# Both FFN output products as seven products of blocks, with the later modulation in the token mixers

## The chip, the cores and the metric

The kernel runs on one core of a Trainium2 chip. A core has TensorE (PE, matmuls; PEld is its weight load), VectorE (DVE), ScalarE (ACT), GpSimd (POOL) and SyncE (SP). Each takes its own list of instructions in order. Here SP issues all the loads and stores. On-chip memory (SBUF) has 128 partitions; matmuls write to PSUM, which has eight banks of 512 float32 numbers a partition. The metric is the device time of one execution in microseconds (us).

## The reference

One layer works on 1024 latent tokens with 1024 features and on 256 context tokens. It has two half-step SwiGLU FFNs with 2816 hidden features, and token mixers between them.

```
x  = x  + 0.5 * ml[2] * swiglu(modulate(rms_norm(x,  norm1_g), ml[0], ml[1]), ffn1_w_in, ffn1_w_out)
cx = cx + 0.5 * mc[2] * swiglu(modulate(rms_norm(cx, norm1_g), mc[0], mc[1]), ffn1_w_in, ffn1_w_out)
hx = modulate(rms_norm(x, norm2_g), ml[3], ml[4])
...            # short gated convolution and attention on hx @ w_in, merged by gates, one output product
x  = x + ml[5] * merge_branches(...)
x  = x + 0.5 * ml[8] * swiglu(modulate(rms_norm(x, norm3_g), ml[6], ml[7]), ffn2_w_in, ffn2_w_out)
return rms_norm(x, final_g)

def swiglu(h, w_in, w_out):
    a, b = jnp.split(h @ w_in, 2, axis=-1)
    return (jax.nn.silu(a) * b) @ w_out
```

The modulation vectors `ml` and `mc` are nine pieces of 1024 numbers, made from `silu(c) @ w_mod + b_mod`. The output products are the ones with `w_out`: 2816 hidden features to 1024 features, for 1024 tokens.

## The kernel before

Features lie in partitions, as 8 tiles of 128 features (22 hidden tiles in the FFNs); tokens lie along the free dimension, in two chunks of 512, C0 and C1. Every float32 operand is split into two float32r parts, hi and lo: ScalarE copies hi, then VectorE subtracts to get lo. A product of tiles takes three matmuls (hi hi, hi lo, lo hi), accumulated in a PSUM bank.

The kernel is traced by Python code, and a scheduler orders each engine's list by its own estimate of times; a few instructions are pinned to the order of the code. Buffers are rings: 38 tiles of 4 KiB a partition in `apool` (`atile`), 11 small tiles in `tpool` (`ttile`), and in `wpool` three buffers for raw weights ("raw") and four each for two parts ("wh", "wl"). PSUM has five banks for products (`ps_s`), two for transposes (`ps_t`) and one more (`ps_o`).

**Input products.** The class `Winograd` already makes the products with `w_in` of both FFNs and most of the mixers' input products by seven products of 2 x 2 blocks where eight would be usual: two tiles of output columns by two halves of input features, and two halves of features by two halves of tokens. One such pair gives a hidden tile for all 1024 tokens. `lefts` makes the left operands (their sums on GpSimd); `norm0` and `norm1` make the right operands of the two token halves; `first`, `second` and `third` make the seven products and add them up on VectorE.

**First FFN.** The loop over the 22 hidden tiles makes the input products. `spill` applies silu and writes the hidden values to DRAM (`hd`). From tile 8 on, the context's products use the same weights. Between the tiles, `run(steps, ...)` issues steps of `all_later_mods`: each loads a row tile of `w_mod` (`rawm`), multiplies and adds it on VectorE (`macc`); after eight such a half of a modulation vector is summed by two small matmuls and comes back as columns through four tiny transfers (`mcol`).

Then come the output products (lines 1029 to 1066). For each chunk the 22 hidden tiles are loaded and split, and so are the residual rows `x`. Feature tiles are taken in groups of 3, 3 and 2; for each, blocks of 8, 8 and 6 row tiles of `ffn1_w_out` are loaded with `load_w`, for both chunks anew. Four steps of the later modulation follow each block in C0; the rest of them follow the first block of C1. The second norm of C0 (`norms2`) is made in four steps while the products of C1 run. Every finished tile is added to `x` under its gate on VectorE, stored to `xd`, and squared for the second norm (`mix.square`, in order of tiles).

**Mixers.** `mix.start(norm1)` begins five pairs while the norm of C1 is made. A loop over 8 feature tiles makes the convolution's inputs and the gates. Values, keys, queries, attention, and the merge follow, unchanged by what is below.

**Second FFN.** `Winograd.ffn` (lines 742 to 786) takes two hidden tiles at a time: their input products, silu, split, and at once their share of the output products for both chunks (8 feature tiles, 2 hidden tiles, 3 parts), added to `x` under the gate. The hidden values never leave the chip. In the last pair C1 is taken in two halves of 256 tokens, and `after2` lets the final norm of what is finished run between them. `final` squares and sums the features of a chunk, makes the scale, transposes back to tokens and stores.

## Time and profile before

| | before |
|---|---|
| median of 3 runs | 2814.75 us (2810.68 to 2815.31) |
| the profiled execution's own time (its span) | 2813.7 us |
| mean granted TensorE clock in it | 0.984 |
| busy: PE, PEld, DVE, ACT, POOL | 2725.5, 2286.0, 1957.2, 1096.5, 542.3 us |
| instructions on PE | 13741 |
| moved by DMA | 298.77 MB, 106 GB/s on average |

The page gives one profiled execution. Busy times count overlapping pieces once, so a busy TensorE need not run at its peak. "Idle before" in a group of instructions is the time its engine stood still just before them, with the instruction that ended the wait. The chain of waits is followed back from the last instruction, so that its shares add up to the span. All helper calls are recorded at line 88, so that rows are told apart by tile names: `ps<-hid,wh` is an output product of the first FFN, `ps<-hid,wo` and `ps<-gh,wo` one of the second, `raw` are raw weights, `macc` is the later modulation.

### The profile page before, as it was taken

How to read it: one execution, taken by the hardware profiler on the slowest of the kernel's cores; microseconds unless marked ns; L12 is line 12 of the kernel's file. 1: busy time of each engine (PE TensorE's matmuls, PEld its weight loads, DVE VectorE, ACT ScalarE, POOL GpSimd, SP SyncE). 2: the span in 40 equal slices, each digit the busy share in tenths (PEclk: the TensorE clock that was granted, in tenths of full speed). 3: DMA queues.
4: the chain of work that ended last, by engine and by line, in shares of the span. 5: the costliest groups of instructions: out<-in, count | busy, mean ns of one | idle time of the engine just before them, and what ended most of it. 6: DMA issues, size and time to landing. Idle time of an engine off the chain costs nothing.

```text
span 2813.7 us, 37012 instructions
## 1 busy us (share of the span) xinstructions
PE 2725.5 (97%) x13741; PEld 2286.0 (81%) x13741; DVE 1957.2 (70%) x3218; ACT 1096.5 (39%) x2176; POOL 542.3 (19%) x433
## 2 busy tenths in 40 slices
PE   7898999999999989999999999999998999999998
PEld 4687988888888868888999888887886788888887
DVE  5886688877864387676568377776458766666667
ACT  3524333333433243333345167764245222232225
POOL 2541122121001054323123000000014221212111
PEclk8899999999999989999999999999999999999999
DMA  8264433445974333323313300002532311221111
GB/s 303 97 199 151 145 111 126 130 142 158 309 236 130 104 119 106 105 69 97 105 46 122 111 23 5 12 1 90 170 93 90 111 41 51 60 60 53 46 53 68
DMA packets 346910, 298.77 MB, mean 106 GB/s; under 512 B 25430, under 2 KB 276456, under 8 KB 346728
## 3 DMA queue, kind: packets, MB, share of 16 engines
q1 hardware_dynamic: 346728, 296.40, 32.9%
q8 instruction: 108, 1.77, 0.3%
q14 instruction: 74, 0.61, 0.1%
HBM read 247.54 MB, written 48.76 MB: 105 GB/s over the span
## 4 chain that ended last, share of the span: by engine, by line
PE 83%; DVE 9%; DMA 3%; issue 2%; ACT 2%; SPq 0%; POOL 0%; ACTq 0%; DVEq 0%; POOLq 0%
PE ps L88 73%; PE po L88 6%; PE pt L88 4%; DVE wl L88 2%; DVE r L88 1%; DVE nt L88 1%; DVE macc L88 1%; DMA raw<-in_ffn_w_out_dram 1%; DMA rawm<-in_w_mod_dram 1%; DVE wo L88 1%; DMA hid<-hd 1%; DVE h L88 1%; DVE uc L88 0%; SPq L88 0%; DMA mcol<-mrow 0%
## 5 line engine op out<-in xcount | busy, mean ns | idle before, releaser
L88 PE MATMUL ps<-r,wl 128*128 128x512 f32 x5280 | 1242.0, 394 | 36.9 <-ACT wl L88 12.8
L88 PEld LDWEIGHTS ps<-r,wl 128*128 128x128 f32 x5280 | 995.5, 190 | 256.1 <-ACT wl L88 16.4
L88 ACT CAST wl<-s 128x512 fp32r<-128x512 f32 x256 | 158.6, 620 | 330.3 <-PE ps L88 274.5
L88 ACT CAST wl<-raw 128x512 fp32r<-128x512 f32 x230 | 142.3, 620 | 245.7 <-PE ps L88 165.8
L88 DVE TENSOR_TENSOR wl<-raw,wl 128x512 fp32r<-128x512 f32 x228 | 167.1, 733 | 99.9 <-ACT wl L88 98.8
L88 DVE TENSOR_TENSOR wl<-s,wl 128x512 fp32r<-128x512 f32 x256 | 217.4, 850 | 11.6 <-ACT wl L88 9.8
L88 POOL TENSOR_TENSOR s<-raw,s 128x512 f32<-128x512 f32 x64 | 99.1, 1549 | 624.2 <-DVE wl L88 618.9
L88 PE MATMUL ps<-hid,wh 128*128 128x512 f32 x704 | 217.2, 390 | 1.4 <-ACT wh L88 1.4
L88 ACT CAST wh<-raw 128x1024 fp32r<-128x1024 f32 (+2 forms) x100 | 97.9, 982 | 251.5 <-PE ps L88 208.6
L88 DVE SCALAR_TENSOR_TENSOR x<-ps,gate_l,x 128x512 f32<-128x512 f32 (+1 forms) x200 | 140.7, 726 | 79.1 <-PE ps L88 78.8
L88 POOL TENSOR_TENSOR sq_acc<-sq_acc,sq 128x512 f32<-128x512 f32 (+1 forms) x33 | 41.8, 1268 | 765.4 <-ACT sq L88 764.6
L88 POOL TENSOR_TENSOR s<-raw 128x512 f32<-128x512 f32 x64 | 91.2, 1424 | 399.4 <-DMA raw<-in_ffn_w_in_dram 164.5
L88 DVE TENSOR_TENSOR wl<-raw,wh 128x1024 fp32r<-128x1024 f32 (+1 forms) x92 | 109.6, 1192 | 67.5 <-ACT wh L88 65.8
L88 PEld LDWEIGHTS ps<-hid,wh 128*128 128x128 f32 x704 | 131.7, 188 | 30.2 <-ACT wh L88 2.6
L88 DVE SCALAR_TENSOR_TENSOR macc<-rawm,silu_c,macc 128x512 f32<-128x512 f32 x168 | 141.4, 859 | 12.0 <-DMA rawm<-in_w_mod_dram 11.0
L88 PE MATMUL ps<-hid,wo 128*128 128x512 f32 (+1 forms) x552 | 147.7, 381 | 0.4 <-DVE x L88 0.3
L88 DVE TENSOR_TENSOR u<-u,ps 128x512 f32<-128x512 f32 x168 | 114.3, 680 | 46.6 <-PE ps L88 46.3
L88 PE MATMUL ps<-wh,r 128*128 128x256 f32 x768 | 141.5, 285 | 0.0
L88 PE MATMUL ps<-gh,wo 128*128 128x512 f32 (+1 forms) x368 | 135.5, 380 | 1.5 <-ACT wo L88 1.5
L88 PE MATMUL ps<-hid,wl 128*128 128x512 f32 x352 | 136.5, 389 | 0.0
L88 DVE TENSOR_REDUCE m<-ps 128x1 f32<-128x512 f32 (+1 forms) x192 | 112.7, 595 | 20.9 <-PE ps L88 19.8
L88 DVE TENSOR_TENSOR pts<-pt,pts 128x512 fp32r<-128x512 f32 x160 | 108.7, 683 | 18.8 <-ACT pts L88 18.4
(259 smaller groups left out, 4897.1 us busy)
## 6 DMA issues: line engine op xcount, KB each, us to landing
raw<-in_ffn_w_in_dram SPq DMA_DIRECT2D x114, 512.0 KB, 3.7
raw<-in_ffn_w_out_dram SPq DMA_DIRECT2D x76, 512.0 KB, 4.6
rawm<-in_w_mod_dram SPq DMA_DIRECT2D x128, 256.0 KB, 4.1
raw<-in_w_in_dram SPq DMA_DIRECT2D x57, 512.0 KB, 4.0
hid<-hd SPq DMA_DIRECT2D x44, 256.0 KB, 6.2
rawm<-in_w_mod_dram SPq DMA_DIRECT2D x16, 512.0 KB, 8.1
xd<-x SPq DMA_DIRECT2D x32, 256.0 KB, 8.6
x<-xd SPq DMA_DIRECT2D x32, 256.0 KB, 6.1
```

The costliest lines, as they stand in the source:

```text
L88: inst = getattr(self.engine, name)(*args, **kw)
```

## The change

The output products of both FFNs are made by one new function, `row_products`, by seven products of blocks. The blocks of `w_out` are halves of its rows (11 hidden tiles each) by halves of its columns (4 feature tiles each). The blocks of the hidden values are the same halves of hidden tiles by the two chunks. Each product has 11 hidden tiles x 4 feature tiles x 3 parts of matmuls, into four banks, where eight products of that size were made before (1056 matmuls for an FFN, now 924). It goes through the hidden tiles in pairs: one load, one split and one block sum handle two row tiles, 1024 elements a partition; the eleventh tile stands alone.

With upper and lower rows u and l, left and right columns, and tokens 0 and 1, the seven products in order are:

| product | left operand (w_out) | right operand (hidden) | goes to |
|---|---|---|---|
| 1 | W(u, left) | B(u, 0) | kept in `chain` |
| 2 | W(l, left) | B(l, 0) | 1 + 2: left tiles, C0 |
| 5 | S = W(u, right) + W(l, right) | T = B(u, 1) - B(u, 0) | left and right tiles, C1 |
| 6 | S - W(u, left) | B(l, 1) - T | 1 + 6: left tiles, C1 |
| 7 | W(u, left) - W(u, right) | B(l, 1) - B(u, 1) | 1 + 6 + 7: right tiles, C1 |
| 4 | W(l, right) | B(l, 1) - T - B(l, 0) | 1 + 6 + 7 - 4: right tiles, C0 |
| 3 | W(l, left) - (S - W(u, left)) | B(l, 1) | left tiles, C1 |

The block sums are made on VectorE in place, in the code of the product before the one that needs them (product 7's left operand is the exception). S stays on the chip; the other weight blocks are loaded when needed: one load a pair in products 1 and 5, three in product 2, two in 7 and 4, none in 6 and 3. All hidden values of 1024 tokens are held at once, as raw float32 in 22 tiles (`Rows`), and are split again for each product.

The second FFN now makes all its hidden values first, writes them to `hd` with `spill`, and reads them back, as the first does. `Winograd.ffn` goes. In its last product tokens are taken in halves of 256 (`halves=True`); the operands of both halves are kept, and the final norm runs between.

The later modulation's steps leave the first FFN's output products: nine go to each of the mixers' eight rounds, and the rest behind them. The second norm of C0 runs during product 3. The squares of C1 are taken in the order in which tiles get done (4 to 7, then 0 to 3). `final` takes one step a feature tile, scales on VectorE, and for 256 tokens gives the sum on TensorE six partial tiles where VectorE added all up before.

```diff
     class Winograd:
...
         def square(self, d):
-            if d == 0:
+            if not self.n_squares:
                 self.acc = [ttile("sq_acc")]
-            sq = self.acc[0] if d == 0 else ttile("sq")
+            sq = ttile("sq") if self.n_squares else self.acc[0]
             act.activation(out=sq, in_=self.xs(d, C1), func=AF.Square)
...
-        def ffn(self, w_o, gate, last_chunks, after):
...
+    class Rows:
+        def __init__(self, n, name):
...
+        def fetch(self, src):
+            for lower in range(2):
+                for c in range(2):
+                    for k, m in self.groups:
+                        j = lower * self.n + k
+                        load(self.t[k, lower, c], src[j : j + m, :, c * 512 : (c + 1) * 512].rearrange("a p n -> p a n"))
+
+    def row_products(w, rows, add, after=lambda i, k: None, halves=False):
+        R, groups = P * rows.n, rows.groups
+        sums = {}
+
+        def part_of_w(k, m, lower, left):
+            t = wpool.tile([P, 2, 512], F32, tag="raw", name=uniq("raw"), bufs=3)[:, :m]
+            o, c = k * P + R * lower, 512 * (not left)
+            load(t, w[o : o + m * P, c : c + 512].rearrange("(a p) n -> p a n", p=P))
+            return t
...
+        def operands(i, k, m, tags=("wl", "wh")):
+            b11, b12, b21, b22 = (rows.t[k, v, c] for v in range(2) for c in range(2))
+            if i == 1:
+                left = part_of_w(k, m, 0, True)
+            elif i == 2:
+                left = part_of_w(k, m, 1, True)
+            elif i == 7:
+                left, a21 = part_of_w(k, m, 0, True), part_of_w(k, m, 0, False)
+                dve.tensor_sub(out=left, in0=left, in1=a21)
+            elif i == 4:
+                left = part_of_w(k, m, 1, False)
+            else:
+                left = sums[k]
+            right = {1: b11, 2: b21, 5: b11, 6: b11, 7: b12, 4: b11, 3: b22}[i]
+            l, r = parts(left, m, tags[0]), parts(right, m, tags[1])
+            if i == 1:
+                dve.tensor_sub(out=b11, in0=b12, in1=b11)
+            elif i == 2:
+                sums[k] = atile("ws", (P, 2, 512))[:, :m]
+                a21, a22 = part_of_w(k, m, 0, False), part_of_w(k, m, 1, False)
+                dve.tensor_add(out=sums[k], in0=a21, in1=a22)
+            elif i == 5:
+                a11 = part_of_w(k, m, 0, True)
+                dve.tensor_sub(out=sums[k], in0=sums[k], in1=a11)
+                dve.tensor_sub(out=b11, in0=b22, in1=b11)
+            elif i == 6:
+                dve.tensor_sub(out=b12, in0=b22, in1=b12)
+            elif i == 7:
+                dve.tensor_sub(out=b11, in0=b11, in1=b21)
+            elif i == 4:
+                a12 = part_of_w(k, m, 1, True)
+                dve.tensor_sub(out=sums[k], in0=a12, in1=sums[k])
+            return l, r
...
+        for i in (1, 2, 5, 6, 7, 4, 3):
...
+            ps = [ps_s() for _ in range(4)]
+            for k, m in groups:
+                steps_of(ps, k, m, *operands(i, k, m))
+                after(i, k)
+            for d in range(4):
+                if i == 1:
+                    chain[d] = ttile("u")
+                    act.copy(out=chain[d], in_=ps[d])
+                elif i == 2:
+                    c = ttile("c")
+                    dve.tensor_add(out=c, in0=chain[d], in1=ps[d])
+                    add(d, C0, c)
+                elif i == 5:
+                    add(d, C1, ps[d])
+                    add(d + 4, C1, ps[d])
...
-    for ch in (C0, C1):
...
+    hs = Rows(NH // 2, "hid")
+    hs.fetch(hd)
+    for k in range(KD):
+        for ch in (C0, C1):
+            sp.dma_start(out=xs(k, ch), in_=xd[k, :, ch[1] : ch[1] + 512])
...
+        if i == 3 and k in (0, 2, 4, 6):
+            run(norms2, 1)
+
+    row_products(ffn1_w_out[0], hs, add1, after1)
...
         run(normc2, 2)
+        run(steps, 9)
...
+    run(steps)
     for k in range(4):
         mix.part_second(k)
...
-    fast.ffn(ffn2_w_out[0], gate3["l"], last_chunks, after2)
+    fast.start(fast.norm1())
+    for j in range(NH):
+        u, c = fast.next_first()
+        v, b = fast.second(u)
+        spill(c, b, j, C0)
+        spill(*fast.third(u, v), j, C1)
+    hs = Rows(NH // 2, "hid")
+    hs.fetch(hd)
...
+    row_products(ffn2_w_out[0], hs, add3, after3, halves=True)
     run(finals[1])
     run(finals[2])
```

More of the change, by code (lines that the diff above doesn't have):

```diff
@@ L480, in __init__ @@
             self.n_ahead, self.side, self.started, self.n_left = ahead, None, [], 0
+            self.n_squares = 0
             self.source, self.ready = self.lefts(pairs, side_from), []
@@ L1065, in tile_dit_layer @@
                 if ch == C1:
                     mix.square(d)
+        if (i, k) == (7, 0):
+            gain2.update(norm_gain("gain2", 3, "g2"))
+            mix.gain = gain2["l"]
+        if k == NH // 2:
+            if i == 2:
+                done(range(4), C0)
+            elif i == 7:
+                done(range(4, KD), C1)
+            elif i == 4:
+                done(range(4, KD), C0)
+            elif i == 3:
+                done(range(4), C1)
+        if i == 3 and k in (0, 2, 4, 6):
+            run(norms2, 1)
```

181 lines of the change are left out of this document (91 added, 90 removed).

## The prediction

> **What bounds the kernel now.** I read the page first, then the stages (busy time by stretches), then the chain of waits, and last the groups and queues inside the two stages that the change rewrites.
>
> ```profile
> span 2813.7 us, 37012 instructions
> PE 2725.5 (97%) x13741; PEld 2286.0 (81%) x13741; DVE 1957.2 (70%) x3218; ACT 1096.5 (39%) x2176; POOL 542.3 (19%) x433
> PE 83%; DVE 9%; DMA 3%; issue 2%; ACT 2%; SPq 0%; POOL 0%; ACTq 0%; DVEq 0%; POOLq 0%
> ```
>
> TensorE is the bound: 97% busy, and 83% of the chain that ended last is its own work. Below are the stages around the change: the first FFN's output products, the start of the mixers, their main loop, most of the second FFN, and the tail after its last output matmul. Columns: stretch, length, busy time and instruction count by engine (PE, PEld, DVE, ACT, POOL), granted clock, DMA share, GB/s.
>
> ```profile
> 724.00:969.50 245.50, 244.09 (x1082) 200.46 (x1081) 131.79 (x176) 83.55 (x113) 12.64 (x7) 1.00 0.62 197
> 969.50:1064.00 94.50, 82.22 (x330) 63.68 (x329) 78.79 (x118) 40.16 (x71) 45.96 (x31) 0.89 0.33 109
> 1064.00:1405.00 341.00, 341.00 (x1619) 287.34 (x1618) 225.39 (x337) 107.78 (x182) 98.28 (x69) 1.00 0.31 98
> 2200.00:2792.80 592.80, 592.38 (x2651) 491.27 (x2651) 397.36 (x579) 168.88 (x290) 110.03 (x82) 1.00 0.17 52
> 2799.30:2813.70 14.40, 6.25 (x38) 5.11 (x37) 6.80 (x26) 7.76 (x18) 1.45 (x2) 0.79 0.52 211
> ```
>
> Both FFN stages run on TensorE without a gap, at full clock. So fewer matmuls there shorten the kernel one for one, as long as the operands keep coming. The other engines have room: VectorE is busy 131.79 of 245.50 us.
>
> **The matmuls saved.** The first FFN's output products are two groups in the list of instructions on the hidden tiles, and one piece of the chain gives their pace:
>
> ```profile
> L88 PE MATMUL ps<-hid,wh x704: 387/389/499, 724.3 to 968.8; 128*128 128x512 f32 x176
> L88 PE MATMUL ps<-hid,wl x352: 388/389/398, 725.9 to 969.1; 128*128 128x512 f32 x176
> 882.39 89.79 PE ps L88 x396
> ```
>
> That is 1056 matmuls (22 hidden tiles x 8 feature tiles x 2 token halves x 3 parts), at 89.79 / 396 = 0.2267 us each: 239.4 us. Seven block products of 11 x 4 x 3 = 132 make 924, so 132 go, 29.9 us. The second FFN saves as many, but its last product is cut into halves of 256 tokens. Two 256-wide matmuls of its present end start one after another:
>
> ```profile
> 2785.86 0.28 PE L88 MATMUL ps<-gh,wo 128*128 128x256 f32 x1
> 2785.98 0.28 PE L88 MATMUL ps<-gl,wo 128*128 128x256 f32 x1
> ```
>
> At 0.12 us, 264 of them take 31.7 us where 132 wide ones took 29.9 (+1.8); the 96 narrow ones there today cost 11.5 against 10.9 (0.6, which goes). Net 29.9 - 1.8 + 0.6 = 28.7 us. Both FFNs together: -58.6 us if nothing waits.
>
> **VectorE and ScalarE in the new stage.** These groups of the first FFN's output stage carry the prices (count, busy, mean ns):
>
> ```profile
> L88 DVE TENSOR_TENSOR wl<-raw,wh 128x1024 fp32r<-128x1024 f32 x32 | 40.1, 1256 | 21.1 <-ACT wh L88 20.5 <-PE pt L88 0.3
> L88 DVE SCALAR_TENSOR_TENSOR macc<-rawm,silu_c,macc 128x512 f32<-128x512 f32 x28 | 21.0, 749 | 2.8 <-DMA rawm<-in_w_mod_dram 2.3
> L88 DVE SCALAR_TENSOR_TENSOR x<-ps,gate_l,x 128x512 f32<-128x512 f32 x15 | 11.2, 747 | 13.1 <-PE ps L88 13.1
> L88 DVE TENSOR_TENSOR u<-u,ps 128x512 f32<-128x512 f32 x168 | 114.3, 680 | 46.6 <-PE ps L88 46.3
> L88 ACT CAST wh<-raw 128x1024 fp32r<-128x1024 f32 x30 | 31.5, 1051 | 61.0 <-PE ps L88 46.5 <-DMA raw<-in_ffn_w_out_dram 14.4
> ```
>
> A pass over 11 tiles is 5.5 operations of 1024 elements, 5.5 x 1.256 = 6.9 us. Each product needs two passes for the low parts of its operands, and eight passes of block sums are spread over the seven: 22 x 6.9 = 152 us. Emptying PSUM adds 16 x 0.68 + 28 x 0.747 = 32 us. That is 184 of 209.5 us (924 x 0.2267): 88% where it was 54%. Products 5 and 7 carry two passes of sums: 4 x 6.9 + 5.7 (4 x 0.68 + 4 x 0.747) = 33 us against 29.9. ScalarE needs 14 x 5.5 x 1.051 = 81 us, about its 83.55 of now. In the second FFN the splits of the halved last product are issued inside product 4: 5 passes + 5.7 = 40 us there, though the last product then needs next to none.
>
> So VectorE fits on the whole, but runs at most two pairs ahead: each pair takes two of four buffers a side. In the built order, product 5's first pairs stand among 4 sums and 4 additions of the product before (5.7 us), and product 6's second operand behind four additions: 2 x 0.747 each side of a 1.256 block sum. I put 3 us of TensorE idle at the turns into 5 and into 6 and 1 us into each of 7 and 4: 8 us per FFN. Bounds: nothing, since two pairs last 2 x 24 x 0.2267 = 10.9 us, and the whole 5.7 us at each of 4 turns, 23 us; I take it near the lower end because evictions stand ahead of most splits. Product 4 in the second FFN: 40 - 30 = 10 at most, 0 at least; 7 us of slack in product 7's stretch go towards it, so 3. The second norm over the first tokens now falls into product 3 of the first FFN: 2 us, between nothing and the 6 us of its eight multiplications.
>
> **Loads.** The queue's own rows and two stretches (PE, clock, DMA share, GB/s):
>
> ```profile
> raw<-in_ffn_w_out_dram SPq DMA_DIRECT2D x76, 512.0 KB, 4.6
> hid<-hd SPq DMA_DIRECT2D x44, 256.0 KB, 6.2
> 737.37 1.40 SPq L88 DMA_DIRECT2D hd<-u x1
> 730.00:740.00 10.00, 10.00 (x46) 1.00 1.07 368
> 740.00:750.00 10.00, 10.00 (x46) 1.00 1.05 389
> ```
>
> All loads are issued by one queue in order. In the changed order the fourth and fifth weight blocks of product 1 stand around the last spill of hidden values (issued at 737.37 today). The sixth stands behind that spill, the rest of the hidden tiles, seven modulation rows and all sixteen rows of x: 8.75 MB, 23 us at 380 GB/s. TensorE wants it 5 x 24 x 0.2267 = 27.2 us after product 1 starts, at 751.5. If the spill goes out by 725, because VectorE no longer splits 23 hidden tiles ahead of it, the block comes in time; if at 737 as now, at 760 plus about 2 us to split. Between 0 and 11 us; I take 4, as the work in front of the spill on VectorE is gone.
>
> Product 2 wants three blocks for each pair from three buffers (its left operand and two for the sum): one round is a landing (4.6), the sum (1.26) and the issue, about 6.3 us against 5.4 us of matmuls for a pair. Five rounds lose some 4 us (0 if the first pairs are early; 5 x 3.5 = 17 us if the landing is that of a crowded queue, 8.1, the median of the 512 KB modulation rows below). I take 4 in the first FFN, and 2 in the second, where neither x nor modulation is loaded. Its start costs 1: the hidden values there are written out and read back, but the first two pairs were prepared long before.
>
> ```profile
> rawm<-in_w_mod_dram SPq DMA_DIRECT2D x16, 512.0 KB, 8.1
> ```
>
> The second FFN's added spill (44 writes, 44 tiles read back) and extra weight reads, 26 MB against 11.5, run at 52 GB/s today and are hidden; the spill leaves the queue behind each tile's product, and the next weights are two hidden tiles ahead.
>
> **What moves.** About 63 steps of the later modulation leave the first output stage for the mixers, with some 26 operations of 0.749 us, their row loads and three column transfers. VectorE has 341.00 - 225.39 = 116 us free there; the row loads share the queue with the mixers' weights. I charge 2 us (between 0 and the 20 us if each were waited for; TensorE has no idle in that stretch now). At the start of the mixers the last product ends with four additions and four squares where two of each stood: 2 us more on a chain that already binds (969.50 to 1064.00). In the tail, rows 4 to 7 are done before and the squares feed the sum on TensorE directly: -1.5 us of 14.4 (bounds 0 and -4).
>
> **The sum**, against the profiled 2813.7 us: first FFN -29.9 + 8 + 2 + 4 + 4 = -11.9; second -28.7 + 8 + 3 + 2 + 1 = -14.7; +2 +2 -1.5. Together -24.1: 2789.6. The median of the three runs, 2814.75, is 1.05 above that execution; so 2790.6. The three runs lie within 0.2%, and 0.2% (5.6 us) is about what a measurement can tell from no change.
>
> **A clock row to weigh.** When TensorE idled 2.69 us, its clock fell in the next stretch:
>
> ```profile
> 598.46 5.75 PE L88 MATMUL ps<-r,wl 128*128 128x512 f32 x17 [2.69 <-ACT u L88]
> 590.00:600.00 10.00, 7.31 (x42) 0.96 0.30 94
> 600.00:610.00 10.00, 10.00 (x55) 0.87 0.20 58
> ```
>
> 0.04 and 0.13 of 10 us: 1.7 us lost beside the gap. [...] It speaks against this change, which trades an unbroken stage for one with turns.
>
> **The rivals.**
> - All of it is hidden: the pairs in hand cover each turn, and no load is late. Then -58.6 and the other terms: 2756 to 2765, say 2763. For it: VectorE at 88%. Against: products 5 and 7 exceed their own stretch. Chance 0.17.
> - The turns trip the clock: the stalls are as I sum them, but at eight turns of 2 us or more the clock drops too, 8 x 1.7 = 14 us: 2804. The gap of 2.69 us speaks for it, and my turns of 1 us against. Chance 0.13.
> - The supply becomes the bound, on the slower side: three raw buffers, filled in order by one queue, are freed only when VectorE reaches the split or the sum, and VectorE's fixed order waits for late tiles with splits behind it. Where a round is 4.6 + 1.05 + 1.26 + 1.26 = 8.2 us, products 2, 7 and 4 (three, two, two blocks for three buffers) take 8.2, 5.5 and 5.5 us per pair; with the crowded landing of 8.1, 11.7, 7.8 and 7.8: 5.5 x (6.3 + 2.4 + 2.4) = 61 us lost per FFN against 29. Halfway between 29 and 61, at 45 us, it gives 2814.75 + 2 x 16 = 2846. It decides from a loss of 29 us per FFN, a landing of about 6.2 us, which the hidden tiles have today. For it: that row; against: 2 of the 7 products are without loads, and one block per pair runs unhindered today at the same landing. Chance 0.22.
> - Nothing to measure: gain and stalls cancel, about 2814. Chance 0.08.
>
> The forecast itself has 0.40. Faster: 0.40 + 0.17 + 0.13 less 0.02 for its spread, 0.68; same 0.08 and a little, 0.09; slower 0.23. The range runs from 2762, the hidden case, to 2832, halfway into the slower one; the likeliest case alone holds 2775 to 2805.
>
> **What would show it.** Right: 924 matmuls in each output stage, PE idle of 15 to 20 us in the first, named after VectorE's splits at the turns and once after a weight load in product 1 or 2; VectorE near 85% there; the mixers' main loop without idle. Wrong: idle before every pair of products 2, 7 and 4 behind in_ffn_w_out loads (supply), clock below 0.95 in the output stages, idle in the mixers behind the modulation's row loads, or no idle at all (the hidden case).

## The result, and the profile after

The changed kernel takes 2830.7 us (median of 4 runs, 2824.8 to 2832.0) where the kernel before takes 2814.8: a ratio of 1.0057, with a 95% interval of 1.0044 to 1.0069. It is slower by 16 us; a gain of 24 us was forecast. The profiled execution took 2829.55 us.

The head of the page of the changed kernel: span, busy time by engine, and the chain that ended last by engine.

```profile
span 2827.5 us, 36964 instructions
PE 2699.5 (95%) x13625; PEld 2258.4 (80%) x13625; DVE 2038.5 (72%) x3214; ACT 1124.7 (40%) x2148; POOL 536.5 (19%) x424
PE 76%; DVE 11%; DMA 6%; issue 2%; ACT 2%; POOL 1%; SPq 1%; DVEq 0%; ACTq 0%; POOLq 0%
```

TensorE has 26 us less to do, and yet the span grew: its share of the chain fell from 83% to 76%, and VectorE's and the DMAs' rose by two and three points. The stages of the changed kernel (columns as in the table of stages before): first FFN's output products, start of the mixers, their main loop, second FFN's output products, tail.

```profile
724.00:965.00 241.00, 222.64 (x942) 177.79 (x940) 189.84 (x219) 90.06 (x108) 6.32 (x3) 0.97 0.48 166
965.00:1064.00 99.00, 77.72 (x288) 59.16 (x289) 80.89 (x120) 45.48 (x82) 45.84 (x31) 0.83 0.34 110
1064.00:1391.00 327.00, 323.79 (x1424) 265.72 (x1423) 249.06 (x367) 107.65 (x181) 105.08 (x73) 1.00 0.36 114
2567.70:2810.60 242.90, 232.06 (x1126) 193.84 (x1125) 176.14 (x209) 85.81 (x107) 0.00 (x0) 0.96 0.38 129
2810.60:2827.50 16.90, 8.50 (x78) 8.05 (x76) 11.08 (x42) 5.85 (x11) 0.00 (x0) 0.93 0.54 218
```

By the marks of single matmuls the time splits into three:

| stage | before, us | after, us | difference | forecast |
|---|---|---|---|---|
| first FFN's output products (to the last of their matmuls) | 245.2 | 239.6 | -5.6 | -11.9 |
| from there through the mixers (to the first context product) | 406.8 | 427.8 | +21.0 | +4 |
| second FFN to the end of the span | 701.6 | 700.2 | -1.4 | -16.2 (with the tail) |

The stretch between the mixers and the second FFN is the same in both kernels (736.0 and 735.9 us). So the question has two halves: why the two output stages gained 7 us instead of 28, and why the mixers, which the change hardly touches, lost 21.

**The output stages.** The output products' groups of the changed kernel in these two stages (first the first FFN, then the second; busy time, mean of one, idle before):

```profile
L88 PE MATMUL ps<-wh,wl 128*128 128x512 f32 x924 | 220.8, 399 | 17.9 <-DVE wh L88 5.8 <-ACT wl L88 5.2 <-DVE u L88 3.3
...
L88 PE MATMUL ps<-wh,wl 128*128 128x512 f32 x792 | 192.7, 403 | 10.8 <-DVE c L88 4.0 <-DVE u L88 2.5 <-DVE wh L88 2.4
L88 PE MATMUL ps<-kept,kept 128*128 128x256 f32 x264 | 34.7, 290 | 0.0
```

There are 924 matmuls, as forecast, and the idle time is as forecast too: 17.9 us in the first stage (18 in the sum: 8 + 4 + 4 + 2) and 10.8 in the second (14). What the sum lacks is in the busy time. At 0.2267 us the 924 would take 209.5 us and took 220.8 (+11.3); the 792 would take 179.5 and took 192.7 (+13.2); the 264 narrow ones would take 31.7 and took 34.7 (+3.0). By these groups matmuls became slower by 27.5 us in all. Some of that is counted twice, because groups overlap where one follows another: all groups of the two stages sum to 223.6 and 236.7 us, and TensorE was busy 222.44 and 232.06. So some 22 us are lost in slow matmuls. The products of the first FFN one by one show where (5, 6, 7 and 4; stretch, length, TensorE busy and count, granted clock, DMA share, GB/s):

```profile
793.00:828.00 35.00, 31.89 (x132) 0.95 0.47 158
828.00:864.50 36.50, 33.02 (x134) 0.95 0.06 19
864.50:895.20 30.70, 29.76 (x130) 1.00 0.50 167
895.20:931.50 36.30, 33.17 (x133) 0.91 0.55 174
```

And the turns into 6, 7 and 4, on TensorE (start, length, operation, count, idle time before it and who ended that):

```profile
831.08 0.50 PE L88 MATMUL ps<-wh,wl 128*128 128x512 f32 x1 [2.46 <-DVE x L88]
832.21 32.12 PE L88 MATMUL ps<-wh,wl 128*128 128x512 f32 x132 [0.63 <-DVE wh L88]
864.96 29.76 PE L88 MATMUL ps<-wh,wl 128*128 128x512 f32 x130 [0.63 <-DVE wh L88]
897.99 1.39 PE L88 MATMUL ps<-wh,wl 128*128 128x512 f32 x2 [3.26 <-DVE u L88]
899.72 32.46 PE L88 MATMUL ps<-wh,wl 128*128 128x512 f32 x132 [0.34 <-DVE wh L88]
```

Behind a gap of 0.63 us the product runs at 0.229 us a matmul; behind 2.46 or 3.26 us it runs at 0.243 to 0.246, and the granted clock of the stretch is 0.95 and 0.91. Set against product 7, each long gap costs its own length and about another 2 us (132 x 0.014 to 0.017); a run below shows that not all of it is the clock's. What ends the gaps is VectorE emptying the PSUM banks of the product before (x, u).

One long gap is not needed, and the clock doesn't always fall. At the turn into 6 of the second FFN three short gaps stand close together, and the product behind them is slow (granted clock 0.95):

```profile
2668.14 0.49 PE L88 MATMUL ps<-wh,wl 128*128 128x512 f32 x1 [0.55 <-DVE x L88]
2669.46 0.51 PE L88 MATMUL ps<-wh,wl 128*128 128x512 f32 x1 [0.82 <-DVE x L88]
2670.59 32.33 PE L88 MATMUL ps<-wh,wl 128*128 128x512 f32 x132 [0.63 <-DVE wh L88]
```

The same turn in a later run (fewer ones-matmuls, below) has the same three gaps (0.55, 0.81 and 0.62 us), the clock stays at 1.00, and the 132 matmuls take 31.07 us instead of 32.33:

```profile
2667.94 31.07 PE L88 MATMUL ps<-wh,wl 128*128 128x512 f32 x132 [0.62 <-DVE wh L88]
```

**The start of the mixers.** TensorE, before and after, from the end of the output products to the ones-matmuls of the norm over the second 512 tokens (pt<-ones):

```profile
969.30 2.88 PE L88 MATMUL ps<-r,wl 128*128 128x512 f32 x12
972.02 0.28 PE L88 MATMUL pt<-ones,sq_acc 128*128 128x1 f32 x2
972.16 2.99 PE L88 MATMUL ps<-r,wl 128*128 128x512 f32 x12
974.99 0.28 PE L88 MATMUL pt<-ones,sq 128*128 128x1 f32 x2
```

```profile
966.02 0.73 PE L88 MATMUL ps<-r,wl 128*128 128x512 f32 x2 [1.42 <-DVE wl L88]
967.28 0.96 PE L88 MATMUL ps<-r,wl 128*128 128x512 f32 x3 [0.53 <-DVE r L88]
969.14 9.22 PE L88 MATMUL ps<-r,wl 128*128 128x512 f32 x27 [0.90 <-DVE r L88]
978.21 0.28 PE L88 MATMUL pt<-ones,sq_acc 128*128 128x1 f32 x2
```

Before, the mixers' first matmuls follow without a gap, and the last of that norm's ones-matmuls are done 7 us after the products. After, there are three gaps behind VectorE's splits (it still makes the norm over the first tokens), 27 matmuls take 9.22 us where they would take 6.1, and the ones-matmuls stand behind 34 product matmuls (two of them ahead of the rows shown) instead of 24: they are done 16 us after the products. In the window to 1064 us TensorE issued 288 instructions in 99 us; before it was 330 in 94.5.

### The profile page after: what moved, and what is told of

The parts are those of the page before. It is cut to its first block, busy times and chain, and to the rows that moved or that the text cites. A ratio compares the mean times of both kernels' runs of the same rounds, so it can differ in the third digit from the quotient of the medians.

```text
span 2827.5 us, 36964 instructions
## 1 busy us (share of the span) xinstructions
PE 2699.5 (95%) x13625; PEld 2258.4 (80%) x13625; DVE 2038.5 (72%) x3214; ACT 1124.7 (40%) x2148; POOL 536.5 (19%) x424
## 4 chain that ended last, share of the span: by engine, by line
PE 76%; DVE 11%; DMA 6%; issue 2%; ACT 2%; POOL 1%; SPq 1%; DVEq 0%; ACTq 0%; POOLq 0%
PE ps L88 67%; PE po L88 6%; DMA raw<-in_ffn_w_out_dram 4%; PE pt L88 4%; DVE wl L88 2%; DMA rawm<-in_w_mod_dram 1%; DVE r L88 1%; DVE macc L88 1%; DVE nt L88 1%; DVE wh L88 1%; SPq L88 1%; DVE x L88 1%; DVE ws L88 1%; DVE h L88 1%; DVE u L88 0%
## 5 line engine op out<-in xcount | busy, mean ns | idle before, releaser
L88 PE MATMUL ps<-wh,wl 128*128 128x512 f32 x1716 | 413.5, 401 | 28.7 <-DVE wh L88 8.2
L88 PEld LDWEIGHTS ps<-wh,wl 128*128 128x128 f32 x1716 | 328.7, 193 | 110.3 <-DVE wh L88 12.8
L88 ACT CAST wl<-raw 128x512 fp32r<-128x512 f32 (+1 forms) x278 | 189.2, 682 | 393.5 <-PE ps L88 256.7
L88 DVE TENSOR_TENSOR wl<-raw,wl 128x512 fp32r<-128x512 f32 (+1 forms) x276 | 221.0, 802 | 122.0 <-ACT wl L88 116.3
L88 POOL TENSOR_TENSOR s<-raw 128x512 f32<-128x512 f32 x64 | 90.8, 1418 | 406.8 <-DMA raw<-in_ffn_w_in_dram 167.8
L88 DVE SCALAR_TENSOR_TENSOR macc<-rawm,silu_c,macc 128x512 f32<-128x512 f32 x168 | 143.4, 872 | 11.6 <-DMA rawm<-in_w_mod_dram 10.7
L88 PEld LDWEIGHTS ps<-wh,r 128*128 128x128 f32 x768 | 120.5, 192 | 0.0
L88 ACT CAST pts<-pt 128x512 fp32r<-128x512 f32 x160 | 93.4, 592 | 64.7 <-PE pt L88 62.3
L88 PE MATMUL po<-pts,vh 128*128 128x512 f32 x256 | 112.4, 440 | 0.4 <-ACT pts L88 0.4
L88 PE MATMUL ps<-kl,qs 128*128 128x512 f32 x384 | 108.3, 399 | 1.3 <-ACT pl L88 1.3
L88 PE MATMUL ps<-wl,r 128*128 128x256 f32 x384 | 108.8, 283 | 0.0
L88 ACT CAST wh<-raw 128x1024 fp32r<-128x1024 f32 (+1 forms) x52 | 51.0, 985 | 139.8 <-PE ps L88 106.4
```

What stands on the lines that cost most here:

```text
L88: inst = getattr(self.engine, name)(*args, **kw)
```

## The experiments

Two theories stood at the start. A: the mixers lose their 20 us for two about equal reasons (the moved modulation steps, and the start), and the output stages gain little because of the turns and the clock after them. Against it: one cause for all, VectorE being full, or a cause that sits in only one of the two FFNs. All kernels are compared with the kernel before in the same session (2812.4 to 2814.3 us). The changed kernel's 2830.7 belongs to a session in which the kernel before took 2814.8, so a difference from 2830.7 is up to 2.4 us too large; where one is given, what is left of it when each kernel is set against its own session stands beside it.

| experiment | median, us | ratio to before | 95% interval |
|---|---|---|---|
| modulation steps back in the products | 2826.2 | 1.0049 | 1.0030 to 1.0068 |
| kernel before with the steps moved alone | 2822.8 | 1.0036 | 1.0023 to 1.0048 |
| first FFN alone | 2833.1 | 1.0073 | 1.0058 to 1.0088 |
| second FFN alone | 2808.7 | 0.9987 | 0.9978 to 0.9997 |
| block sums on GpSimd | 2876.1 | 1.0226 | 1.0211 to 1.0242 |
| late additions | 2818.6 | 1.0021 | 1.0011 to 1.0030 |
| filled turns, order held widely | 2842.0 | 1.0103 | 1.0086 to 1.0120 |
| filled turns | 2826.7 | 1.0044 | 1.0028 to 1.0061 |
| norm before product 4 | 2823.4 | 1.0043 | 1.0028 to 1.0057 |
| late additions, second FFN alone | 2809.3 | 0.9979 | 0.9970 to 0.9989 |
| steps from the fourth round | 2821.0 | 1.0025 | 1.0016 to 1.0034 |
| mended | 2810.2 | 0.9987 | 0.9977 to 0.9996 |
| fewer ones-matmuls | 2821.0 | 1.0026 | 1.0017 to 1.0036 |
| banks end apart | 2829.2 | 1.0052 | 1.0038 to 1.0067 |
| second FFN alone, mended | 2803.3 | 0.9959 | 0.9945 to 0.9973 |
| mended, fewer ones-matmuls | 2800.8 | 0.9956 | 0.9943 to 0.9968 |
| the same, filled turns | 2802.2 | 0.9959 | 0.9945 to 0.9973 |

### Which half of the change costs

The first FFN's half alone (the changed kernel with the second FFN of before), and the second FFN's half alone (the kernel before with the changed second FFN and tail).

> The changed kernel with the second FFN and the final norm of the kernel before: the seven products in the first FFN alone, and the moved modulation. Theory A (the first FFN's side, mixers included, costs 15 us, the second FFN gains 1.4): 2830 to 2834. Rival (the second FFN is what loses, by its round trip through DRAM): 2815 to 2824.

> The kernel before with the second FFN and the final norm of the changed kernel alone. Theory A: 2811 to 2816, a gain within the noise. Rival (the second FFN loses): 2822 or more. The forecast of the second FFN, which gains 14.7 us and 1.5 in the tail, would have it at 2798 to 2800.

2833.1 and 2808.7: the first FFN's half costs 20.7 us against its session's 2812.4, the second gains 3.7. They add up to 17, about what the whole change costs (16). So the loss lies on the first FFN's side, with the mixers behind it, and the second FFN's products win, though not the 15 us of the forecast.

### The moved modulation steps

```diff
 in the mixers (and the closing run(steps) there)
-        run(steps, 9)
 in after1
+        if i in (2, 5) and k < NH // 2:
+            run(steps, 4)
+        if (i, k) == (6, 0):
+            run(steps)
```

> The changed kernel, with the later modulation's steps back beside the first FFN's output products (four after each pair of products 2 and 5, the rest in product 6) and none in the mixers. Theory A (the mixers lose 20 us for two reasons of about equal size: the norm of the second tokens starts 8 us later, and the moved steps stall the first round): the mixers get back 8 to 10 us, the output stage loses 3 to 8 to the busier VectorE, 2820 to 2828. Theory B (the moved steps alone cost the 20 us): 2808 to 2814. Theory C (the moved steps cost nothing): 2831 or more.

The other way round, the kernel before with its steps moved into the mixers in the same way and nothing else:

> The kernel before, with only the later modulation moved: none beside the first FFN's output products, nine steps in each round of the mixers and the rest behind them. Theory A: 2820 to 2826 (8 to 10 us in the mixers, little back in an output stage that already runs on TensorE). Theory B: 2832 or more. Theory C: 2812 to 2816.

2826.2 and 2822.8. Moving the steps alone costs the kernel before 10 us. Taking them back into the new products gives only 4.5 (2.1 by sessions), no more than the spread of its runs, 2818.1 to 2833.4. VectorE has more to do there then, 199.83 us from 724 to 965 us instead of 189.84, and TensorE issues 901 instructions in that time instead of 942. The chain of waits of the kernel before with the steps moved, in the mixers' first rounds:

```profile
1058.34 4.61 DMA yd<-y
...
1068.95 5.66 DMA rawm<-in_w_mod_dram
1074.64 0.66 DVE macc L88
```

The rows of the modulation's weights are waited for on VectorE, in order, with the mixers' next splits behind them. If that is a matter of place, the steps cost nothing further on:

```diff
-        run(steps, 9)
+        if i >= 3:
+            run(steps, 14)
```

> The changed kernel with the moved modulation steps begun in the mixers' fourth round (14 in each) instead of its first (9 in each). Theory B (the moved steps cost some 10 us only where they stand: in the first two rounds VectorE waits in order for rows of the modulation weights while it has the mixers' splits behind them; later rounds have VectorE's slack): 2820 to 2825 us. Rival (any round stalls by about as much, since the rows come through the same queue): 2828 to 2833 us.

2821.0, which is 9.7 us less (8.2 by sessions), at the better end of theory B. From the end of the output products to the first context product this run takes 417.3 us, 10.5 less than the changed kernel and 10.5 more than the kernel before: the moved steps are one half of the 21 us, and the start is the other. It isn't that the waits vanish. In the changed kernel and in this one VectorE's idle time before these operations is

```profile
  DMA rawm<-in_w_mod_dram: 5.8, 4
```

```profile
  DMA rawm<-in_w_mod_dram: 3.6, 3
```

(us, times). But from 1064 to 1384 us TensorE is busy 319.29 us in this run, and 316.79 in the changed kernel. I read it so: in the first two rounds nothing is prepared ahead, and the waits reach TensorE; from the fourth round on products are ahead, and such waits cost nothing to speak of.

### The start of the mixers

The second norm over the first 512 tokens one product earlier:

```diff
-        if i == 3 and k in (0, 2, 4, 6):
+        if i == 4 and k in (0, 2, 4, 6):
```

> The changed kernel with the second norm over the first 512 tokens taken in product 4 instead of 3, so before product 4's share is in x (the output is no longer the reference's). Theory A (the mixers lose some 8 to 10 us because VectorE does the second half of that norm at the end of product 3, so that the norm over the second 512 tokens starts 15 us after the products instead of 7): the mixers' first matmuls come 6 to 10 us earlier, product 4 loses up to 3 us: 2820 to 2827 us. Rival (the start waits for the second tokens' own four additions and squares, or for the weights' splits): 2828 to 2833 us.

2823.4, which is 7.3 us less (5.4 by sessions; this kernel's norm leaves out product 4's share). That is inside theory A's range, but not by its mechanism. TensorE there:

```profile
967.73 11.83 PE L88 MATMUL ps<-r,wl 128*128 128x512 f32 x50
979.40 0.28 PE L88 MATMUL pt<-ones,sq_acc 128*128 128x1 f32 x2
1005.93 1.22 PE L88 MATMUL ps<-r,wl 128*128 128x512 f32 x2 [8.19 <-ACT wl L88]
```

The mixers now start without a gap and at full clock (1.00 from 967.8 to 981 us; 0.77 from 965 to 980 in the changed kernel), 50 matmuls in 11.83 us where the changed kernel needed 12.3 us for 32. But the second tokens' norm does not begin earlier: its ones-matmuls stand behind 50 product matmuls instead of 34, at 979.4 us, and a longer wait follows (8.19 us; 6.41 in the changed kernel). So the norm's place costs some 4 us (18 matmuls) through VectorE's late splits and the clock after the gaps; the late second norm stays, and it goes with TensorE's order, which no run changed alone.

Next, the four banks of product 3 ending 2 us apart:

```diff
+            if i == 3:
+                both = [(k, m, *operands(i, k, m)) for k, m in groups[-2:]]
+                for d in range(4):
+                    for g in both:
+                        steps_of(ps, *g, ds=(d,))
```

> The changed kernel with product 3 of the first FFN ending feature tile by feature tile: its last two pairs of tiles are done for one bank after the other, so that the banks end 2 us apart instead of 0.7, and nothing else. Theory S (the mixers start late because four additions, four squares and their sums stand behind the last matmul): the norm over the second tokens starts 3 to 5 us earlier, 2824 to 2828 us. Rival (it is late because VectorE and ScalarE still work on the norm of the first tokens then, whatever the order of the banks): 2829 to 2832 us.

2829.2, the rival's (1.5 us less, and nothing by sessions). The four additions and squares at the end aren't what the start waits for; the norm's first operation on VectorE comes 15.8 us after the products here, and 16.3 in the changed kernel.

### The turns

Three ways to treat the gaps. First, VectorE is relieved of the block sums:

```diff
 eight times in operands()
-                dve.tensor_sub(out=b11, in0=b12, in1=b11)
+                pool.tensor_sub(out=b11, in0=b12, in1=b11)
```

> The changed kernel with the eight block sums of each FFN's output products on GpSimd instead of VectorE. Theory A (VectorE's work at the turns between products makes PE idle and the clock falls behind each gap): 8 passes of 6.9 us, 55 us a stage, leave VectorE, the gaps into products 5, 6 and 4 shrink from about 3.5 us to under 1.5 us each, the clock stays near 1.0: 2805 to 2818 us against 2830.7. Rival (GpSimd, 1.74 us per 512 elements in the mixers, some 3.5 us per block sum, is too slow for products 5 and 7, which hold two passes: 38 us of sums in 30 us of matmuls): new gaps behind GpSimd's sums, 2829 to 2846 us.

2876.1, worse than even the rival allowed. The right operands' splits on VectorE in the changed kernel, and then splits on VectorE and a block sum on GpSimd in this one (count, busy, mean ns, in the first output stage):

```profile
L88 DVE TENSOR_TENSOR wh<-hid,wh 128x1024 fp32r<-128x1024 f32 x35 | 42.7, 1219 | 1.5 <-ACT wh L88 1.5
```

```profile
L88 DVE TENSOR_TENSOR wh<-hid,wh 128x1024 fp32r<-128x1024 f32 x34 | 57.3, 1685 | 8.7 <-ACT wh L88 8.7
L88 DVE TENSOR_TENSOR wl<-ws,wl 128x1024 fp32r<-128x1024 f32 x15 | 28.9, 1925 | 6.6 <-ACT wl L88 6.6
...
L88 POOL TENSOR_TENSOR hid<-hid,hid 128x1024 f32<-128x1024 f32 x20 | 56.0, 2811 | 44.9 <-DMA mcol<-mrow 29.1 <-DVE wh L88 9.8 <-DMA x<-xd 3.0
```

The sums take 2.8 us there instead of 1.22, and the splits that stayed on VectorE become 38 to 58% longer. VectorE gave away eight passes and had hardly more time for it: from 724 to 965 us it was busy 185.61 us instead of 189.84. So this run doesn't tell what a VectorE with less to do would be worth.

Second, the banks are copied out by ScalarE and the additions to x come later:

```diff
                 steps_of(ps, k, m, *operands(i, k, m))
+                late(k == (0 if i == 3 else 2))
 ...
+            if i not in (1, 3):
+                for d in range(4):
+                    t = ttile("pc")
+                    act.copy(out=t, in_=ps[d])
+                    ps[d] = t
```

> The changed kernel with each product's four PSUM banks (2, 5, 6, 7, 4) copied out by ScalarE at once, and the additions to x issued on VectorE behind the next product's second pair of tiles (first pair in product 3) instead of ahead of it. Theory A1 (the gap at a turn is VectorE emptying PSUM, four sums and four additions of 0.7 us ahead of the next splits): gaps into 5, 6 and 4 fall to under 1 us in both FFNs and the clock with them: 2808 to 2820 us. Rival A2 (the gap is the operands' splits, which come late because VectorE is full over the whole product): the gaps stay, at another place, 2826 to 2838 us.

2818.6: 12 us (10.3 by sessions), in the range of theory A1, though its picture is only half right. The gaps are not gone; as rival A2 had it, they stand at another place, further inside the next product, behind a split (second FFN, products 5, 6 and 7):

```profile
2630.67 32.05 PE L88 MATMUL ps<-wh,wl 128*128 128x512 f32 x132 [2.28 <-DVE wh L88]
2665.26 32.02 PE L88 MATMUL ps<-wh,wl 128*128 128x512 f32 x132 [2.54 <-DVE wh L88]
2698.52 25.17 PE L88 MATMUL ps<-wh,wl 128*128 128x512 f32 x108 [1.24 <-DVE wh L88]
```

Behind 2.28 and 2.54 us the clock falls as before (0.95 over the product), behind 1.24 us it does not (1.00, 0.233 us a matmul). By the forecast's sum products 5 and 7 still ask more of VectorE than their own length holds. The same on the kernel before, second FFN alone:

> The kernel before with the second FFN alone as in the changed kernel, and there the PSUM banks copied by ScalarE and the additions to x behind the next product's second pair. Theory A1 (emptying PSUM ahead of the splits costs the second FFN its gain; the late additions gave 5.5 us there beside the first FFN's 8): 2801 to 2806 us, faster than before. Rival (the second FFN's turns are independent of the place of the additions): 2807 to 2812 us as with the second FFN alone.

2809.3 against 2808.7 without the late additions, which is the rival's range. The second FFN's stretch is 4 us shorter in the profiled executions (693.1 against 697.1), but this one was the fastest of its ten (2804.2), and the medians show nothing: inconclusive. Its trace holds the counterpart to the gap of 2.54 us above. Here the clock stays at 1.00 behind as long a gap, and the product takes 1.6 us less, 30.43 instead of 32.02:

```profile
2654.24 30.43 PE L88 MATMUL ps<-wh,wl 128*128 128x512 f32 x132 [2.55 <-DVE wh L88]
```

Third, TensorE is kept busy at the turns with ten matmuls whose results nobody reads:

```diff
+            if i in ((2, 7) if halves else (2, 5, 7)):
+                po, (wh, _), (xh, _) = ps_o(), *ops
+                for r in range(10):
+                    matmul(po, wh[:, 0, :P], xh[:, 0], start=r == 0, stop=r == 9, pinned=True)
```

> The changed kernel with ten extra matmuls (their results unused, 2.3 us) on TensorE at the end of products 2, 5 and 7 of the first FFN and 2 and 7 of the second, where it waits for VectorE now; the matmuls at the edges of a product keep the written order. Clock theory (after a gap of 2.5 to 4 us the clock falls, and the next 132 matmuls take 32.1 to 32.8 us instead of 29.9): with the gaps filled they take 30 to 30.5, five turns x 2.0 to 2.5 us: 2818 to 2823 us. Rival (the slower stretch comes from other things, such as single waits too short to be seen): no gain, and fillers that delay the next product: 2829 to 2836 us.

2842.0, which neither theory had. To place the fillers this kernel also held the first and last pairs of all products in the written order, the last product's too, and so the final transposes went in between its matmuls: its last twelve came at 2822 instead of 2809 us. So its time says nothing on the clock. With only the two matmuls beside each filler held, and in both FFNs three turns:

> The changed kernel with ten extra matmuls (results unused, 2.3 us) on TensorE between products 2 and 5, 5 and 6, 7 and 4 of both FFNs, only these and the two matmuls beside them held in the written order; elsewhere the order is the changed kernel's. Clock theory (after a gap of 2.5 to 4 us the next 132 matmuls take 32.1 to 32.8 us; after a filled turn they took 30.3 us in the run before): five turns x 2 to 2.5 us: 2818 to 2823 us. Rival (the time belongs to VectorE, and TensorE at full clock only reaches the next wait sooner): 2827 to 2833 us.

2826.7, between the two. In the trace the clock theory holds where a turn was filled (into 6 and into 4 of the first FFN):

```profile
830.34 2.43 PE L88 MATMUL po<-wh,wl 128*128 128x512 f32 x10
832.61 0.84 PE L88 MATMUL ps<-wh,wl 128*128 128x512 f32 x3
833.73 31.07 PE L88 MATMUL ps<-wh,wl 128*128 128x512 f32 x132 [0.28 <-DVE wh L88]
...
897.06 1.55 PE L88 MATMUL ps<-wh,wl 128*128 128x512 f32 x3
899.24 30.68 PE L88 MATMUL ps<-wh,wl 128*128 128x512 f32 x132 [0.63 <-DVE wh L88]
```

The 132 matmuls take 31.07 and 30.68 us instead of 32.12 and 32.46, and the clock over the two products is full (stretch, length, TensorE busy and count, granted clock, DMA share, GB/s):

```profile
833.70:864.90 31.20, 30.89 (x132) 1.00 0.07 22
899.20:930.00 30.80, 30.59 (x132) 1.00 0.58 184
```

So the clock's part is 1.1 and 1.8 us a turn rather than 2 to 2.5; the rest of the slower pace was not the clock's. Into 5 new short gaps came instead, and the median gained 4 us (2.4 by sessions) of the 8 to 13 expected.

### The tail

```diff
-            if k % 2 and (k > 4 or n == 512):
+            if sqs and (k % 2 and k > 4 or o < 768):
                 dve.tensor_add(out=sq, in0=sq, in1=sqs.pop())
```

> The changed kernel with the final norm's squares of the first two chunks added up to one tile on VectorE, and so 6 ones-matmuls (of two passes) for them instead of 28; the last chunk as it is. Theory T (the tail's part of the missing gain is TensorE's own time: 57 of these passes stand among the last products and take 6.6 us): 44 passes of 0.115 us fewer, 2825 to 2828 us. Rival (the additions on VectorE, which also empties the last product, delay the end by as much): 2829 to 2834 us.

2821.0: 9.7 us (8.1 by sessions), more than the 3 to 6 of theory T. The ones-matmuls from product 4 to the end, after and here:

```profile
L88 PE MATMUL pt<-ones,sq 128*128 128x1 f32 x80 | 9.3, 243 | 0.0
```

```profile
L88 PE MATMUL pt<-ones,sq 128*128 128x1 f32 x36 | 4.4, 234 | 0.0
```

The 4.9 us are as worked out. The other 3 to 5 aren't explained by the edit: in that execution the turn into 6 kept its clock (31.07 us instead of 32.33, the rows above), and the matmuls of product 4 ran faster (393 ns instead of 414). No run says why.

### Put together

The kernel before with the second FFN mended (filled turns, fewer ones-matmuls), then the changed kernel with the late additions, the steps from the fourth round, the norm one pair earlier and the banks apart; the same with fewer ones-matmuls; and that with fillers as well:

> The kernel before with the second FFN alone as in the changed kernel (2808.65 us with that alone), with filled turns there and the final sums of the run with fewer ones-matmuls. If the clock and the tail each give what their traces show (3 us and 3 to 5 us): 2800 to 2804 us, faster than before by 0.4%. Rival (each gain moves into the next wait): 2806 to 2811 us.

> The changed kernel with the late additions in both FFNs, the modulation steps from the fourth round, the second norm over the first tokens one pair of tiles earlier, and product 3 of the first FFN ending feature tile by feature tile (its last two pairs), so that its four banks are emptied 2 us apart. If the three causes add up (late additions -12, moved steps -8, start of the mixers -5): 2803 to 2808 us, faster than before. Rival (they share the same waits, or the mixers' start waits for the norm whatever the end of product 3): 2811 to 2818 us.

> The mended kernel (late additions, modulation steps from the fourth round, norm of the first tokens earlier, product 3 ending bank by bank) with the final sums of fewer ones-matmuls too. If the parts add up: 2810.2 - 9.7 = 2800 us (2798 to 2803), at least level with the kernel before with the second FFN mended (2803.3), so that the first FFN's products win a little too. Rival (the late additions had taken the same time out of the tail): 2806 to 2811 us.

> The same with eight extra matmuls (1.8 us) between products 2 and 5, 5 and 6, 7 and 4 of both FFNs. With the late additions the gaps stand further inside the next product, behind a split. Clock theory: a shorter rest of the gap, clock kept, 3 to 5 us under the run without them. Rival (gaps inside the product can't be filled at the turn; six fillers of 1.8 us only add): 0 to 10 us over it.

2803.3, 2810.2, 2800.8 and 2802.2. The first came out as the theory had it, and so did the third: 2810.2 - 9.7 = 2800.5. The second lies between theory and rival: the parts sum to 2805 to 2808 and gave 2810. Fillers add nothing beside the late additions. The mended kernel beats both by 0.44% (0.32 to 0.57) and 1%, with the change's mathematics. Its first output stage:

```profile
L88 PE MATMUL ps<-wh,wl 128*128 128x512 f32 x924 | 218.7, 396 | 16.1 <-DVE wh L88 9.0 <-ACT wl L88 6.4 <-DVE wl L88 0.4
```

Even there 16.1 us are idle and 9.2 lost in slow matmuls. From the first matmul to the end of the output projection it is only 1.4 us ahead of before (2110.7 against 2112.1), while its second FFN takes 687.8 us against 701.6. So the first FFN's seven products about break even with the mixers' dearer start; the gain is in the second.

## Why the prediction was wrong

The direction was wrong, and one rival describes more of the result than the forecast does. Of the 38 us between the forecast and the profiled execution 17 are the mixers', 15 the second FFN's with the tail and 6 the first FFN's output products. Step by step:

- **The matmuls saved** (-29.9 and -28.7): right. 924 each, and the 0.2267 us hold within about 1% where the clock is full and no wait cuts in (0.229 in product 7 of the first FFN).
- **The turns and the waits in products 1 and 2** (18 and 14 us of idle): about right in sum, 17.9 and 10.8, and partly by luck: in the first FFN the 8 us for the turns were 11, the 8 for products 1 and 2 were 5.6, and the 2 for the norm were none. Right in kind too: VectorE's emptying of PSUM and its splits at the turns, short waits for weights in product 2, none in 7 and 4 (the supply did not become the bound). The forecast put 1 us into each of 7 and 4; 0.6 and 3.6 were measured. VectorE was busy 79% of the first stage (189.84 of 241 us), where 85 to 88% was forecast.
- **The clock**: this is the step that failed in the output stages. The sum charged gaps at their own length. The rival that did charge it (eight turns at 1.7 us, 14 us for both FFNs, chance 0.13) had the mechanism: of some 22 us of slower matmuls, the granted clock of 0.97 and 0.96 over the two stages accounts for 7 and 10 (3% of 241.0 us, 4% of 242.9). The forecast set it aside because its turns were 1 us at two of the four places; three of the six turns in the first FFN and two in the second hold a gap of over 2.4 us, and a third turn of the second holds three short ones. Part of the other 5 us is, as an estimate, the restart after each wait: a single matmul behind a wait shows as 0.49 to 0.51 us in the rows of the turns, and one in a row adds 0.23; I did not separate the two further. The traces have the drop behind a gap of 3.26 us (0.91 over product 4) and behind shorter ones: 0.95 over the products behind 2.28, 2.46 and 2.54 us here, and 0.96 and 0.87 in the two stretches at the 2.69 us of the forecast's own row.
- **The moved modulation** (+2, bounds 0 and 20): mis-sized. It costs about 10 us (10.4 alone on the kernel before, 8.2 to 9.7 won back by moving it on), and the reason given was wrong: that VectorE has 116 us free in the mixers says nothing of the first two rounds. Begun in the fourth round, it costs about what was forecast. The sum also left out that these steps' own TensorE passes (8 of 0.4 us) leave the first output stage: -29.9 + 17.9 + 10.1 of slow matmuls (11.3 less the 1.2 counted twice) = -1.9, and these 2 to 3 us with the 1.4 us of idle that the stage had before make the way to -5.6.
- **The start of the mixers** (+2): mis-sized as well, and the place was wrong. The four additions and squares at the end cost nothing that could be measured (banks apart: 0 to 1.5 us less, within the spread). About 8 of its 10.5 us are lost by 1064 us without the moved steps (315 instructions in 99 us instead of 330 in 94.5): 3.4 + 4.5. About 4 of them are the gaps behind VectorE, which still makes the first tokens' norm, and the clock after them; the rest I put down to the ones-matmuls' later place in TensorE's order. That was not tried alone and stays open.
- **The norm in product 3** (+2): the forecast looked at product 3 and not behind it. It caused no idle time there, but its multiplications run past the end of the stage.
- **The tail** (-1.5): wrong sign. The last product's end to the end of the span takes 16.9 us instead of 14.4, and feeding the squares straight to TensorE puts 9.3 us of ones-matmuls on the engine that is the bound. Undone for two of the three chunks, the kernel is 8 to 10 us faster, of which 4.9 are those passes.

The second FFN with the tail closes by the engine's totals from its first matmul to the end of the span. TensorE was idle 22.2 us before and 31.4 after; 8.9 of these 9.2 us are the output products' waits, 10.8 now and 1.9 before. It was busy 679.0 and 668.4 us, 10.6 less: of the 28.7 saved, 11.6 went into slow matmuls (16.2 less the 4.6 counted twice) and 7.4 into ones-matmuls (32 passes before, 96 now). The rest is within 1 us. So of the saving the waits, which the sum had, and the slow matmuls and ones-matmuls, which it had not, leave the measured 1.4.

What the forecast said would show it wrong did show: a clock under 0.95 in the stretch of product 4, and idle in the mixers behind the modulation's rows.

## What to carry to other kernels

A gap on the bound engine is not charged at its length alone: look for rows behind gaps of that size in the trace, and take the slower matmuls that follow as a term of its own; here it was some 22 us beside 28.7 us of gaps. When steps move into a stage with free time, look at the round they land in, not at the stage's average: the same DMA-fed steps on an in-order engine cost about 10 us when begun in the first round and next to nothing from the fourth. And work taken from a busy engine is not saved if the engine that gets it slows the first: VectorE gave eight passes to GpSimd and was busy 185.61 us of the first stage instead of 189.84.

## What the runs showed of the hardware

- VectorE's splits became 38 to 58% longer (1219 to 1685, 1222 to 1925 ns) while GpSimd worked on tensors in SBUF beside it, and GpSimd's sums took 2811 ns on the mean. In the same trace a split of 1024 columns took 1.21 us at 806.5 us, when GpSimd stood still, and 3.41 us at 811.7 us, when a GpSimd sum that had begun at 810.65 ran until 814.0. The forecast of that run had counted GpSimd's own time alone.
- The length of one gap does not settle whether the clock drops. In the first 5 us behind a gap the granted clock was 1.00 after 1.85 us (product 2 of the changed kernel, at 771.12 us) and 0.66 after 1.80 us (the tail of the kernel before, at 2803.06 us; 1.00 just ahead of that gap); the product behind 2.54 us had 0.95 and the one behind 2.55 us 1.00 (late additions in both FFNs, and in the second alone). Three gaps of 0.55, 0.82 and 0.63 us close together were followed by 0.95 in one execution and by 1.00 in another. Behind 1.24 us standing alone it was 1.00 (late additions, product 7 of the second FFN).
- Filling a gap with useless matmuls kept the clock at 1.00 over the next product and gave back 1.1 and 1.8 us a turn, and 2 to 4 us of the kernel's time.
